# Gate products of the expert layer: sixteen tokens in one batch, and their steps as separate background tasks

## The chip, the cores and the metric

The kernel runs on one core of a Trainium2 chip. The metric is the time of one execution in device microseconds (us); lower is better. A core has TensorE (PE, matrix multiplications; PEld are its weight loads), VectorE (DVE), ScalarE (ACT), GpSimd (POOL) and SyncE (SP, which here only issues loads). Each engine works through its own list of instructions in order; semaphores join the lists.

## The reference, cut to what matters

Two blocks of a transformer run one after the other on 256 tokens of width 1024. The first block has two layers, and each of them ends in an expert layer ("peer") with 16384 experts; the change is in that one. For every token, eight heads choose 16 experts each and a softmax weight (the gate) for each.

```
hid = gelu(einsum('td,thkd->thk', tc, u[ec]))
return einsum('thk,thkd->td', gc * hid, v[ec])
```

`ec` holds the indices of the chosen experts (a number from 0 to 16383, made of two halves e1 and e2 of 7 bits each), `gc` the gates, `u` and `v` the tables of experts.

## The kernel before, in words

**The expert layer is computed densely.** All 16384 experts are multiplied, since 256 tokens choose 32768 of them in all. First the U phase: 128 tiles of `u`, each 128 experts by 1024; TensorE multiplies a tile with all 256 tokens, ScalarE applies gelu, and H (in two buffers, `Ha` and `Hb`, expert by token) stands in SBUF. Then the V phase: H is multiplied by the gates, and 128 tiles of `v` are multiplied with it and summed in four PSUM banks (`acc`).

**Every tile of weights comes the same way** (class `Weights`). SP loads 512 KB into `wraw` (three buffers), ACT rounds it to `whi` (L178), DVE subtracts to get the rest `wlo` (L179); both have three buffers, and `W.get()` of a tile first splits the tile two ahead. A product in near-fp32 precision is three matmuls, hi by hi, hi by lo, lo by hi (L320 to L322). A tile is 24 of them. In the V phase the moving operand is split as well: `gated` multiplies H of one row of experts by its gates (L1018, DVE, from a buffer `gj` that POOL fetches from DRAM), and `hg` splits it into `xh` (L333, ACT) and `xl` (L334, DVE), two tiles ahead.

**Gates.** For tokens 0 to 127 the gates are scattered to a DRAM table and fetched back (`gj`). For tokens 128 to 255 they are made on chip, and that is the function `gates(half, newps, cost)`: for every token, a one-hot matrix of e1 (`ga`, 128 wide) times a one-hot matrix of e2 scaled with the gate (`gbh` and `gbl`, the gate's high and low half in f16, 64 columns for one half of the experts). It works in groups of eight tokens, 16 groups to a half, and has three steps:

- `make(q)`: four operations on 128 x 512 or 128 x 1024 values in f16. `gb` (L965) and `ga` (L966) on DVE; `gbh` (L967) and `gbl` (L968) on DVE in half 0 and on POOL in half 1. `gb` has one buffer, the others two.
- `mult(q)`: sixteen matmuls of 64 columns (L975, L976) into a PSUM bank, on TensorE, between two weight tiles.
- `fold(q)`: DVE multiplies H by the bank (L985).

Half 0 is called in the U phase of each layer, at its tile 72, and half 1 at the start of the V phase: four stretches in the program, with 16 groups each.

**What sets the order.** A queue of background tasks, `bg`, holds pairs of a cost and a function. After each weight tile `bg.tick(rate)` adds `rate` to a credit and runs tasks while the credit is above zero, taking each one's cost from it. `rate` is the sum of all costs divided by the number of tiles to spread them over (54 in half 0, 60 in half 1). Before, a task is `step(q)` with a cost of 1.0: `mult(q-1)`, then `make(q)`, then `fold(q-2)`; there are 18 of them for 16 groups, so a step runs after every third tile, in half 1 sometimes after a fourth.

Of the kernel before, what the change touches and what calls it, by code (L numbers as in the profile page):

```python
# [248 lines left out]
def _program(tc, nc, glob, wpool, mmp, accp, drp, ins, out, scat, stop):  # L249
# [33 lines left out]
    bg = Tasks()  # L283
# [3 lines left out]
    def zero(l, src, upto):  # L287

        n = 128 * 128 // NZ
        while cleared[l] < min(upto, NZ):  # L290
            i = cleared[l]
            nc.scalar.dma_start(scat[l][:, i * n:i * n + n], src)
            cleared[l] += 1
# [19 lines left out]
    def mmtile():  # L313
        return mmp.tile([128, 512], F32, tag="mm", name="mm")
# [165 lines left out]
    def ft_tile(ps, n, cols=None, first=True, steady=True):  # L480

        hi, lo = W.get()
        if first and steady:
            settle(ps)
        for c in range(8):
            s = slice(c * 128, c * 128 + 128)
            xh_, xl_ = n.x(c, cols)
            mm3(ps, hi[:, s], lo[:, s], xh_, xl_, first and c == 0, c == 7, skip_group_check=True)
# [269 lines left out]
    def peer(l, n, close_parts, open_parts):  # L758
# [191 lines left out]
        bg.add(0.4, to_hk)  # L950


        def gates(half, newps, cost):
            st = {}

            E = nc.gpsimd if half else V

            def make(q):
                s = slice(q * 8, q * 8 + 8)
                js = slice(half * 64, half * 64 + 64)  # L960
                a = sp.tile([128, 8, 128], F16, name="ga", bufs=2)
                b = sp.tile([128, 8, 64], F16, name="gb", bufs=1)
                bh = sp.tile([128, 8, 64], F16, name="gbh", bufs=2)
                bl = sp.tile([128, 8, 64], F16, name="gbl", bufs=2)
                V.tensor_tensor(b, n8[:, None, js].to_broadcast([128, 8, 64]), e2T[:, s, None].to_broadcast([128, 8, 64]), op=ALU.is_equal)  # L965
                V.tensor_tensor(a, n8[:, None, :].to_broadcast([128, 8, 128]), e1T[:, s, None].to_broadcast([128, 8, 128]), op=ALU.is_equal)  # L966
                E.tensor_tensor(bh, b, gh[:, s, None].to_broadcast([128, 8, 64]), op=ALU.mult)  # L967
                E.tensor_tensor(bl, b, gl[:, s, None].to_broadcast([128, 8, 64]), op=ALU.mult)  # L968
                st[q] = (a, bh, bl)

            def mult(q):
                a, bh, bl = st.pop(q)
                ps = newps()
                for t in range(8):
                    T_.matmul(ps[:, t * 64:t * 64 + 64], a[:, t], bh[:, t], start=True, stop=False)  # L975
                    T_.matmul(ps[:, t * 64:t * 64 + 64], a[:, t], bl[:, t], start=False, stop=True)  # L976
                P.broken = False
                st[("p", q)] = ps

            def fold(q):  # L980
                pv = st.pop(("p", q)).rearrange("p (t j) -> p j t", t=8)
                t = slice(128 + q * 8, 128 + q * 8 + 8)
                for j0, j1 in ((0, NA), (NA, 64)) if half == 0 else ((64, 128),):
                    hv = Ha[:, j0:j1, t] if j1 <= NA else Hb[:, j0 - NA:j1 - NA, t]
                    V.scalar_tensor_tensor(hv, pv[:, j0 - half * 64:j1 - half * 64], 1.0 / GSCALE, hv, op0=ALU.mult, op1=ALU.mult)  # L985

            def step(q):
                if 0 <= q - 1 < 16:
                    mult(q - 1)
                if q < 16:  # L990
                    make(q)
                if 0 <= q - 2 < 16:
                    fold(q - 2)

            for q in range(18):
                bg.add(cost, lambda q=q: step(q))


        xn = Plain(xh, xl)
# [24 lines left out]
        def hg(upto):  # L1024
            gated(upto)
            while done[0] <= min(upto, 127):
                j = done[0]
                split(xh[:, j % 8, 0:256], xl[:, j % 8, 0:256], Ha[:, j] if j < NA else Hb[:, j - NA])
                done[0] += 1

        rate = TK_U
        for jp in range(64):
            if jp == TK_G // 2:
                bg.drain()
                gates(0, acctile, 1.0)
                rate = bg.spread(126 - TK_G)
            ps = mmtile()
            for s in range(2):
                ft_tile(ps[:, s * 256:s * 256 + 256], xn, slice(ROW - SEQ, ROW), s == 0)
                bg.tick(rate)  # L1040
            if l == 0:
                zero(1, zt, jp + 1)
            if jp == 63:
                bg.drain()
                hg(1)
            j = jp * 2
            A.activation(Haf[:, j * 256:j * 256 + 512] if j < NA else Hbf[:, (j - NA) * 256:(j - NA) * 256 + 512], ps, AF.Gelu)  # L1047


        gates(1, mmtile, 1.0)  # L1050
        rate = bg.spread(TK_V)
        acc = [acctile() for _ in range(4)]

# [501 lines left out]
    if stop == "mix0":  # L1555
        dump()
        return close_parts()
    n = peer(0, nxt, close_parts, lambda: open_parts(lambda pr, sp: Norm(("norm_mix", 1), META, pr, mmtile)))
    if stop == "peer0":
        dump()  # L1560
# [7 lines left out]
    if stop == "mix1":  # L1568
        dump()
        return close_parts()  # L1570
    n = peer(1, made["n"], close_parts, lambda: open_parts(lambda pr, sp: TwoNorms(pr, sp, mmtile), ROW))
    btp = tc.tile_pool(name="btp", bufs=1)
    sp = btp.__enter__()
# [50 lines left out]
```

## Time and profile before

| what | value |
|---|---|
| median of 3 runs | 2392.7 us (2392.18 to 2393.62) |
| the profiled execution | 2391.17 us, span of its instructions 2389.4 us |
| TensorE | busy 2362.6 us, 99% of the span, 20554 matmuls |
| VectorE | busy 1839.7 us, 77% |
| ScalarE | busy 1208.0 us, 51% |
| GpSimd | busy 644.7 us, 27% |
| granted TensorE clock | 0.998 of full speed |

TensorE is busy nearly all the time and its chain ends last: 92% of the chain of waits is TensorE's. A busy TensorE is not one at its peak, because matmuls overlap and their ends are modelled; the distance from one start to the next tells what a matmul takes. The times of the trace count from the start of the span. The four stretches with gates lie at about 399 to 547 us and 1269 to 1417 us (half 0) and at 561 to 724 us and 1431 to 1594 us (half 1).

### The profile page before, as it was taken

The page shows a single profiled execution, that of the slowest core. Times are in us where ns is not written, and L with a number is a line of the kernel's source. Part 1 is how long each engine was busy: PE and PEld are TensorE (multiplying, and loading weights), DVE is VectorE, ACT ScalarE, POOL GpSimd, SP SyncE. Part 2 cuts the span into 40 slices and gives each one's busy share as a digit, 9 for nine tenths or more (in the row PEclk, how much of TensorE's full clock was granted, in tenths as well). Part 3 has the DMA queues.
Part 4 walks back from the last instruction along what each step waited for, and adds up shares of the span by engine and source line. Part 5 has one row for each costly group of instructions (what it writes and reads, how often), then busy time and mean ns, then how long its engine had stood idle before and what let it go on. Part 6 is the DMA issues. An engine that isn't in the chain of part 4 may idle for free.

```text
span 2389.4 us, 50610 instructions
## 1 busy us (share of the span) xinstructions
PE 2362.6 (99%) x20554; PEld 2302.4 (96%) x20554; DVE 1839.7 (77%) x3518; ACT 1208.0 (51%) x1753; POOL 644.7 (27%) x421
## 2 busy tenths in 40 slices
PE   8999999999999999999999999999999999999999
PEld 6799999999999999999999999999999998789999
DVE  6689896887996668798987879986677655767774
ACT  4555555444444555555554444445565443446553
POOL 0007877812330000038878504310010000200000
PEclk9999999999999999999999999999999999999999
DMA  7578888765666665657777756666665565325655
GB/s 246 164 245 228 230 224 205 179 191 194 206 207 220 220 216 191 206 167 179 186 178 188 191 185 200 205 215 220 220 197 186 177 175 181 118 98 178 195 191 170
DMA packets 170650, 464.39 MB, mean 194 GB/s; under 512 B 52368, under 2 KB 54424, under 8 KB 169904
## 3 DMA queue, kind: packets, MB, share of 16 engines
q1 hardware_dynamic: 117440, 420.04, 54.9%
q0 software_dynamic: 43616, 24.27, 8.0%
q10 hardware_dynamic: 9360, 16.84, 1.9%
q8 instruction: 161, 2.64, 0.4%
q14 instruction: 73, 0.60, 0.1%
HBM read 443.09 MB, written 17.99 MB: 193 GB/s over the span
## 4 chain that ended last, share of the span: by engine, by line
PE 92%; DVE 6%; ACT 1%; issue 1%; DMA 1%; SPq 0%; ACTq 0%; DVEq 0%
PE mm L320 19%; PE mm L322 19%; PE mm L321 19%; PE acc L320 10%; PE acc L321 10%; PE acc L322 9%; PE acc L258 3%; PE mm L258 2%; DVE wlo L179 2%; DMA wraw<-in_mix_in 1%; PE acc L262 0%; ACT whi L178 0%; PE mm L975 0%; PE acc L975 0%; PE mm L976 0%
## 5 line engine op out<-in xcount | busy, mean ns | idle before, releaser
L179 DVE TENSOR_TENSOR wlo<-wraw,whi 128x1024 fp32r<-128x1024 f32 (+2 forms) x799 | 995.3, 1249 | 399.6 <-ACT whi L178 388.9
L178 ACT CAST whi<-wraw 128x1024 fp32r<-128x1024 f32 (+2 forms) x799 | 834.6, 1045 | 618.4 <-PE mm L321 214.4
L320 PE MATMUL mm<-xh,whi 128*128 128x256 f32 (+1 forms) x2632 | 739.1, 281 | 0.0
L322 PE MATMUL mm<-xh,wlo 128*128 128x256 f32 (+1 forms) x2632 | 732.1, 278 | 1.2 <-DVE wlo L179 1.1
L321 PE MATMUL mm<-xl,whi 128*128 128x256 f32 (+1 forms) x2632 | 731.5, 278 | 0.0
L320 PE MATMUL acc<-xh,whi 128*128 128x256 f32 x2048 | 568.6, 278 | 0.5 <-ACT xh L333 0.5
L321 PE MATMUL acc<-xl,whi 128*128 128x256 f32 x2048 | 565.8, 276 | 0.2
L322 PE MATMUL acc<-xh,wlo 128*128 128x256 f32 x2048 | 565.5, 276 | 0.0
L887 POOL DMA_INDIRECT gates<-gt,idx x256 | 483.4, 1888 | 217.8 <-DVE idx L877 94.5
L320 PEld LDWEIGHTS mm<-xh,whi 128*128 128x128 f32 x2632 | 495.1, 188 | 7.3 <-issue 6.4
L322 PEld LDWEIGHTS mm<-xh,wlo 128*128 128x128 f32 x2632 | 495.2, 188 | 2.6 <-DVE wlo L179 2.2
L321 PEld LDWEIGHTS mm<-xl,whi 128*128 128x128 f32 x2632 | 497.6, 189 | 0.0
L320 PEld LDWEIGHTS acc<-xh,whi 128*128 128x128 f32 x2048 | 384.5, 188 | 0.9 <-ACT xh L333 0.9
L321 PEld LDWEIGHTS acc<-xl,whi 128*128 128x128 f32 x2048 | 384.7, 188 | 0.5 <-DVE xl L334 0.5
L322 PEld LDWEIGHTS acc<-xh,wlo 128*128 128x128 f32 x2048 | 384.5, 188 | 0.0
L322 PE MATMUL mm<-ph,wlo 128*128 128x256 f32 (+1 forms) x800 | 226.1, 283 | 4.3 <-DVE wlo L179 4.3
L320 PE MATMUL mm<-ph,whi 128*128 128x256 f32 (+1 forms) x800 | 227.1, 284 | 0.0
L321 PE MATMUL mm<-pl,whi 128*128 128x256 f32 (+1 forms) x800 | 225.8, 282 | 0.0
L322 PEld LDWEIGHTS mm<-ph,wlo 128*128 128x128 f32 x800 | 151.1, 189 | 4.7 <-DVE wlo L179 4.7
L321 PEld LDWEIGHTS mm<-pl,whi 128*128 128x128 f32 x800 | 151.6, 190 | 0.3
L320 PEld LDWEIGHTS mm<-ph,whi 128*128 128x128 f32 x800 | 151.3, 189 | 0.1
L1047 ACT ACTIVATE Hb<-mm 128x512 f32<-128x512 f32 x112 | 67.0, 598 | 164.8 <-PE mm L322 154.6
(333 smaller groups left out, 3027.3 us busy)
## 6 DMA issues: line engine op xcount, KB each, us to landing
wraw<-in_u SPq DMA_DIRECT2D x256, 512.0 KB
wraw<-in_v SPq DMA_DIRECT2D x256, 512.0 KB
wraw<-in_ffn_in SPq DMA_DIRECT2D x88, 512.0 KB
wraw<-in_mix_in SPq DMA_DIRECT2D x52, 512.0 KB
gates<-zt ACTq DMA_DIRECT2D x64, 256.0 KB
wraw<-in_wq SPq DMA_DIRECT2D x32, 512.0 KB
gj<-gates POOLq DMA_DIRECT2D x64, 256.0 KB
wraw<-in_ffn_out SPq DMA_DIRECT2D x32, 512.0 KB
```

The lines of the kernel that those rows point to most:

```text
L178: self.nc.scalar.copy(hi[:, :cols], raw[:, :cols])
L179: self.nc.vector.tensor_tensor(lo[:, :cols], raw[:, :cols], hi[:, :cols].bitcast(F32), op=ALU.subtract)
L258: return T_.matmul(*a, **k)
L320: T_.matmul(ps, wh, mh, start=start, stop=False, **kw)
L321: T_.matmul(ps, wh, ml, start=False, stop=False, **kw)
L322: T_.matmul(ps, wl, mh, start=False, stop=stop, **kw)
L887: b = nc.gpsimd.indirect_dma_start(out=flat, out_offset=bass.IndirectOffsetOnAxis(ap=idx[:, i:i + 1], axis=0), in_=gt0[:, i:i + 1], in_off ...
L1047: A.activation(Haf[:, j * 256:j * 256 + 512] if j < NA else Hbf[:, (j - NA) * 256:(j - NA) * 256 + 512], ps, AF.Gelu)
```

## The change

`gates` loses its parameter `cost`, and `step` is gone. Groups go in pairs: five tasks for two groups, with costs of their own (0.5, 0.8, 0.3, 0.2, 0.2; 2.0 for a pair and 16 for a half). Both `mult` of a pair stand in one task, so their 32 matmuls follow each other. The sizes of the operations, the buffers and the engines stay as they are.

```
-        def gates(half, newps, cost):
+        def gates(half, newps):
...
-            def step(q):
-                if 0 <= q - 1 < 16:
-                    mult(q - 1)
-                if q < 16:
-                    make(q)
-                if 0 <= q - 2 < 16:
-                    fold(q - 2)
-
-            for q in range(18):
-                bg.add(cost, lambda q=q: step(q))
+            for q in range(0, 16, 2):
+                bg.add(0.5, lambda q=q: make(q))
+                bg.add(0.8, lambda q=q: make(q + 1))
+                bg.add(0.3, lambda q=q: (mult(q), mult(q + 1)))
+                bg.add(0.2, lambda q=q: fold(q))
+                bg.add(0.2, lambda q=q: fold(q + 1))
...
-                gates(0, acctile, 1.0)
+                gates(0, acctile)
...
-        gates(1, mmtile, 1.0)
+        gates(1, mmtile)
```

The lines below `step` move up by four: L1018 of before is L1014 now.

VectorE in the V phase, half 1, before: one whole step and the tiles up to the next one (`gb` and `ga` make a group, L985 folds an older one, then a tile's own L1018, L179 and L334 follow).

```order
L965 TENSOR_TENSOR gb<-n_1331,e2T 128x512
L966 TENSOR_TENSOR ga<-n_1331,e1T 128x1024
L985 SCALAR_TENSOR_TENSOR Hb<-mm,Hb 128x64x8
L1018 TENSOR_TENSOR Ha<-Ha,gj 128x128
L179 TENSOR_TENSOR wlo<-wraw,whi 128x1024
L334 TENSOR_TENSOR xl<-Ha,xh 128x256
```

VectorE at the same stage now, in the third pair of the half.

```order
L965 TENSOR_TENSOR gb<-n_1331,e2T 128x512
L966 TENSOR_TENSOR ga<-n_1331,e1T 128x1024
L1014 TENSOR_TENSOR Hb<-Hb,gj 128x128
L179 TENSOR_TENSOR wlo<-wraw,whi 128x1024
L334 TENSOR_TENSOR xl<-Hb,xh 128x256
L965 TENSOR_TENSOR gb<-n_1331,e2T 128x512
L966 TENSOR_TENSOR ga<-n_1331,e1T 128x1024
L1014 TENSOR_TENSOR Hb<-Hb,gj 128x128
L179 TENSOR_TENSOR wlo<-wraw,whi 128x1024
L334 TENSOR_TENSOR xl<-Hb,xh 128x256
```

The second `make` now stands one tile behind the first, and no fold stands behind `ga`. In half 1 this is so in four of the eight pairs of a layer; in the other four there are two tiles between the makes. From one pair to the next there are seven or eight tiles. `mult` of a pair stands three tiles behind the second `make` (in half 0 twice only two), the folds one or two tiles behind `mult`. In half 0 the makes of a pair stand one tile apart in four pairs and two tiles apart in four.

GpSimd at the start of half 1, before: a fetch of `gj` stands between the products of two groups.

```order
L967 TENSOR_TENSOR gbh<-gb,gh 128x512
L968 TENSOR_TENSOR gbl<-gb,gl 128x512
L1008 DMA gj<-gates 128x512
L967 TENSOR_TENSOR gbh<-gb,gh 128x512
L968 TENSOR_TENSOR gbl<-gb,gl 128x512
```

GpSimd at the same place now.

```order
L967 TENSOR_TENSOR gbh<-gb,gh 128x512
L968 TENSOR_TENSOR gbl<-gb,gl 128x512
L967 TENSOR_TENSOR gbh<-gb,gh 128x512
L968 TENSOR_TENSOR gbl<-gb,gl 128x512
L1004 DMA gj<-gates 128x512 x2
```

The products of a pair follow each other, and the fetches stand behind both.

## Rows read from the trace of the kernel before

**Rows 1.** The page, part 1: busy us, share of the span, instructions.
```profile
PE 2362.6 (99%) x20554; PEld 2302.4 (96%) x20554; DVE 1839.7 (77%) x3518; ACT 1208.0 (51%) x1753; POOL 644.7 (27%) x421
```

**Rows 2.** PE's waits, all of those for wlo: total us, times, longest.
```profile
PE mm L322 <- DVE wlo L179: 5.4, 5, 2.1
```

**Rows 3.** Timeline of PE, first matmuls behind a gate batch: start, us, operation.
```profile
407.68 0.37 PE L320 MATMUL mm<-xh,whi 128*128 128x256 f32 x1
407.88 0.28 PE L321 MATMUL mm<-xl,whi 128*128 128x256 f32 x1
```

**Rows 4.** Timeline of DVE (start, us), first step of half 1: no fold.
```profile
561.54 0.68 DVE L965 TENSOR_TENSOR gb<-n,e2T 128x512 f16<-128x512 f16 x1
...
563.28 1.13 DVE L1018 TENSOR_TENSOR Ha<-Ha,gj 128x128 f32<-128x128 f32 x1
564.33 2.06 DVE L179 TENSOR_TENSOR wlo<-wraw,whi 128x1024 fp32r<-128x1024 f32 x1
566.31 0.41 DVE L334 TENSOR_TENSOR xl<-Ha,xh 128x256 fp32r<-128x256 f32 x1
566.65 0.28 DVE L1018 TENSOR_TENSOR Ha<-Ha,gj 128x128 f32<-128x128 f32 x1
```

**Rows 5.** Timeline of POOL: products of the first two groups of half 1.
```profile
562.40 1.86 POOL L967 TENSOR_TENSOR gbh<-gb,gh 128x512 f16<-128x512 f16 x1 [69.18 <-DVE gb L965]
564.23 1.08 POOL L968 TENSOR_TENSOR gbl<-gb,gl 128x512 f16<-128x512 f16 x1
...
570.83 3.75 POOL L967 TENSOR_TENSOR gbh<-gb,gh 128x512 f16<-128x512 f16 x1 [5.00 <-PE mm L976]
574.55 1.03 POOL L968 TENSOR_TENSOR gbl<-gb,gl 128x512 f16<-128x512 f16 x1
```

**Rows 6.** Timeline of DVE, second step of half 1: no fold behind it.
```profile
569.99 0.68 DVE L965 TENSOR_TENSOR gb<-n,e2T 128x512 f16<-128x512 f16 x1
...
571.73 0.28 DVE L1018 TENSOR_TENSOR Ha<-Ha,gj 128x128 f32<-128x128 f32 x1
...
573.07 0.42 DVE L334 TENSOR_TENSOR xl<-Ha,xh 128x256 fp32r<-128x256 f32 x1
573.40 0.28 DVE L1018 TENSOR_TENSOR Ha<-Ha,gj 128x128 f32<-128x128 f32 x1
574.62 2.05 DVE L179 TENSOR_TENSOR wlo<-wraw,whi 128x1024 fp32r<-128x1024 f32 x1 [0.93 <-ACT whi L178]
```

**Rows 7.** Timeline of DVE, a later step, with its fold.
```profile
590.27 0.69 DVE L965 TENSOR_TENSOR gb<-n,e2T 128x512 f16<-128x512 f16 x1
...
592.01 0.68 DVE L985 SCALAR_TENSOR_TENSOR Hb<-mm,Hb 128x512 f32<-128x512 f32 x1
...
595.04 0.41 DVE L334 TENSOR_TENSOR xl<-Ha,xh 128x256 fp32r<-128x256 f32 x1
```

**Rows 8.** Timeline of PE: the first use of the xl of rows 7.
```profile
596.43 0.28 PE L321 MATMUL acc<-xl,whi 128*128 128x256 f32 x1
```

**Rows 9.** Timeline of ACT, a V tile without gates: its whi.
```profile
734.55 1.05 ACT L178 CAST whi<-wraw 128x1024 fp32r<-128x1024 f32 x1 [1.36 <-PE acc L321]
```

**Rows 10.** Timeline of DVE, V tiles without gates.
```profile
736.78 0.42 DVE L334 TENSOR_TENSOR xl<-Hb,xh 128x256 fp32r<-128x256 f32 x1
737.11 0.28 DVE L1018 TENSOR_TENSOR Hb<-Hb,gj 128x128 f32<-128x128 f32 x1
738.35 1.23 DVE L179 TENSOR_TENSOR wlo<-wraw,whi 128x1024 fp32r<-128x1024 f32 x1 [0.95 <-ACT whi L178]
739.50 0.42 DVE L334 TENSOR_TENSOR xl<-Hb,xh 128x256 fp32r<-128x256 f32 x1
```

**Rows 11.** Busy time of a half-1 stretch: PE, PEld, DVE, ACT, POOL, clock, DMA.
```profile
560.00:720.00 160.00, 160.00 (x1585) 159.41 (x1584) 149.18 (x213) 78.27 (x112) 56.14 (x46) 1.00 0.64 205
```

**Rows 12.** Timeline of DVE, U phase: a make without a fold.
```profile
399.23 0.69 DVE L965 TENSOR_TENSOR gb<-n,e2T 128x512 f16<-128x512 f16 x1
...
402.17 2.58 DVE L179 TENSOR_TENSOR wlo<-wraw,whi 128x1024 fp32r<-128x1024 f32 x2
```

## The prediction, made before the changed kernel was run

> **What bounds the kernel now.** I read the page's busy times first, then TensorE's waits, then the timelines of TensorE, VectorE and GpSimd in the four stretches with gates. TensorE is busy for 99% of the span [rows 1], and its waits for `wlo` come to 5.4 us in all [rows 2]; none of them lies in a gate stretch. So time is won only by taking work from TensorE, and lost as soon as an operand of the next tile comes too late. The reader is to see how much room there is for that. In half 1 VectorE is busy 149.2 of 160 us [rows 11], and in a tile of 24 matmuls everything is due at a fixed point.
>
> **How late VectorE may be.** A V tile takes 2.72 us (L334 of one tile to the next, 736.78 to 739.50 [rows 10]). ACT's `whi` starts when TensorE frees its buffer, some 0.13 us into a tile that starts at 734.42 [rows 9]. Call this tile 0. Its program position makes `xl` of tile 2, which ends at 736.78 + 0.42 = 737.20, so 2.78 us after the start of tile 0. Tile 2 starts 5.44 us after it and reads `xl` with its second matmul, 0.11 later. The room is 5.55 - 2.78 = 2.8 us. A regular step before uses most of it: from rows 7, `xl` ends at 595.04 + 0.41 = 595.45, and its first use is at 596.43 [rows 8]; 0.98 us are left. A step is followed by two or three tiles without one, each of which gives back some 1.05 us (2.72 less the 1.67 us that L1018, L179 and L334 take, 571.73 to 573.40 [rows 6]), so nothing ever waits.
>
> **The change part by part.**
>
> *What it removes.* A batch of 64-column matmuls has a cost of its own where it ends: the first weight matmul behind it takes 0.20 us to the next start (407.68 to 407.88 [rows 3]) where one takes 2.72 / 24 = 0.113 elsewhere. That is 0.09 us, and 64 batches become 32: 32 x 0.09 = **-2.9 us**. The matmuls themselves stay. All operations on the other engines stay too, in number and size.
>
> *What it moves, half 1.* Two makes stand close together, and no fold stands behind `ga`. The price of such a make is seen twice in the trace, and the two differ.
>
> - First step of half 1: `gb` starts at 561.54, and L1018 of the next tile at 566.65, so a make and the tile's own work take 5.11 us; `xl` ends at 566.31 + 0.41, 5.18 us after `gb` [rows 4]. Without a make that is 1.67. L1018 takes 1.13 instead of 0.28 and `wlo` 2.06 instead of 1.23: each stands while one of GpSimd's products runs (562.40 to 564.26 and 564.23 to 565.31 [rows 5]).
> - Second step: 569.99 to 573.40 is 3.41 us, `xl` ends 3.50 us after `gb` [rows 6], and nothing is slow. GpSimd's `gbh` takes 3.75 us instead [rows 5]: it gets on only when VectorE pauses at 573.7, and `wlo` behind the pause is slow (2.05).
>
> So VectorE and GpSimd exclude each other here, and a make costs 1.74 us on VectorE and about 1.7 us more, at once or later. In a step with a fold 0.60 of it runs beside the fold, which does not stand still (0.68 [rows 7], its usual time).
>
> The Trainium skill, page "SBUF — State Buffer", section "Who interferes with whom", says that a VectorE instruction with two SBUF inputs and a GpSimd instruction that reads SBUF exclude each other for a whole instruction, and that the one issued first goes first. By that rule GpSimd would go first in every pair, as in rows 4. Rows 6 disagree: `gbh` was issued at 570.83, and four VectorE instructions issued after it passed.
>
> I take rows 4 for the forecast: GpSimd's second product got in directly behind L1018 in the first step too, and in every regular step (all have a slow `wlo`); rows 6 are the exception.
>
> Pairs one tile apart (four in a layer): the first `gb` starts with the tasks of tile 0, at 737.11 - 734.42 = 2.69. The second stands 5.11 later, at 7.80. The `xl` behind it ends 5.18 later, at 12.98; it belongs to tile 4, due at 10.88 + 0.11 = 10.99. TensorE waits **2.0 us**.
>
> Pairs two tiles apart (four in a layer): two folds stand one tile ahead; their 1.2 us, with the 0.20 of L1018, overrun the 1.24 between L1018 and the next `wlo` (737.11 to 738.35 [rows 10]), which makes the start some 0.16 late: 2.85. Then 5.11 and a plain tile of 1.67 give 9.63, `xl` ends at 14.81, due at 13.60 + 0.11. TensorE waits **1.1 us**.
>
> After the wait there are seven or eight tiles at 1.05 us of gain each to the next pair, so lateness doesn't add up. The sum of half 1 is 2 layers x (4 x 2.0 + 4 x 1.1) = **+24.8 us**.
>
> The bounds of this. Below: where GpSimd finds pauses and VectorE pays 1.74 a make, `xl` of a close pair ends at 2.69 + 3.41 + 3.50 = 9.6, before 10.99, and nothing waits: 0. Above: the order of rows 6 in every second make. The second `gb` needs the buffer of the first, so VectorE stands until both products are through (573.40 to 575.58, 2.2 us [rows 5, 6]): second `gb` at 2.69 + 3.41 + 2.2 = 8.3, `xl` ends at 11.8, 0.8 late. Then GpSimd waits for VectorE's next pause, which comes only after it has caught up, some three tiles of 1.67 on, at about 16; the products end at 18. `mult` is due behind tile 4, at 13.6 + 0.8 = 14.4, so TensorE waits 3 us or more there. That makes 3.8 a close pair and about 2.8 a wide one, 2 x (4 x 3.8 + 4 x 2.8) = 53 us.
>
> *GpSimd's queue.* The fetch of `gj` now stands behind both products of a pair. It is issued four tiles (10.9 us) before its use; two makes hold it up by some 5 us in rows 4's order. I cost it at nothing; with rows 6's order the cover is nearly gone, which is part of the 53.
>
> *What it moves, half 0.* All four operations of a make are VectorE's: 2.94 us (399.23 to 402.17 [rows 12]). Two makes (5.88) and two `wlo` (1.14 each) are 8.2 us against three tiles of 8.16. Depending on where gelu delays `whi`, a close pair is just in time or 0.2 late. I take **+0.5 us** (bounds 0 and 2). `mult` of a pair comes at least two tiles (5.4 us) behind the second make, against 2.94 of work; the folds stand behind `mult` by at least a tile, whose `wlo` can't start earlier than `mult` does. Both cost nothing.
>
> *The sum.* 2391.2 of the profiled execution - 2.9 + 24.8 + 0.5 = 2413.6. The median is 1.5 above that execution, so **2415 us**, some 0.9% slower.
>
> **The rivals.**
>
> 1. *GpSimd starves* (rows 6 in most second makes): 2391.2 - 2.9 + 53 + 0.5 = 2442, at the median 2443. For it speaks that the second step is the nearer likeness, with GpSimd already at work in the half; against it that the other hand-overs went to GpSimd.
> 2. *Not slower.* GpSimd's products run wholly in VectorE's pauses and beside folds, and the second `gb` finds its buffer free. Then only the 2.9 us are left: 2390. It decides at the second `gb`: it holds if VectorE has paused 2.2 us between the two makes. The pauses of a plain tile are 0.95 us [rows 10]; a close pair has one tile between, a wide one two. So this speaks against it.
> 3. *A part of it.* The order changes from pair to pair so that the wide pairs lose nothing and the close ones 1 to 1.5 us: 2 x 4 x 1.2 = 10, so 2400. For it speaks that DVE idles and DMA landings move the phase between pairs.
>
> **How the numbers follow.** What can't be told from no change here is 0.2%, 4.8 us. Forecast 2415 (rows 4's order): 0.50, its own range 2407 to 2424. Rival 1: 0.25. Rival 3: 0.14. Rival 2: 0.11; of that 0.08 within 0.2%, 0.03 faster by more, since 2.9 us is all that the trace shows to be won. The range for 8 times in 10 is 2398 to 2441: from just below rival 3 to about rival 1. Slower by over 0.2%: 0.89.
>
> **What would show it.** 32 batches of 32 matmuls with one slow first matmul behind each. In half 1, TensorE waits eight times per layer of 1 to 2 us, for `xl` of the fourth tile that starts behind a close pair's first make and the fifth behind a wide pair's; L1018 and `wlo` at 1.13 and 2.06 behind both makes of a pair. Half 0 with next to no waits. Rival 1 would show in `gbh` of over 3 us and waits at L975 for GpSimd. The prediction is wrong if TensorE runs through the close pairs without a wait, or if the loss lies in half 0 or outside the four stretches.

## The result, and the profile after

The changed kernel takes 2426.2 us (median, 2423.32 to 2428.16), the kernel before 2392.44 (2390.41 to 2393.62) in the runs beside it: ratio 1.0141, interval 1.0127 to 1.0155. Forecast were 2415 us and a range of 2398 to 2441: slower as forecast, within the range, and 11 us more than the value. The profiled executions took 2427.13 us (span 2425.4) and 2391.17 (span 2389.4), so 36.0 us are to be explained.

Part 1 of the page after (busy us, share of the span, instructions):

```profile
PE 2376.2 (98%) x20554; PEld 2313.0 (95%) x20554; DVE 1853.7 (76%) x3518; ACT 1205.1 (50%) x1753; POOL 672.4 (28%) x421
```

The counts are those of before [rows 1]: nothing was added or left out. The first three of TensorE's waits of after (total us, times, longest):

```profile
PE acc L321 <- DVE xl L334: 19.2, 16, 1.5
PE mm L258 <- ACT whi L178: 9.8, 1, 9.8
PE mm L322 <- DVE wlo L179: 5.2, 4, 2.1
```

The last line is [rows 2] again, and the middle one stood in the kernel before with 8.2 us. The first is new: sixteen waits for `xl`, eight in each layer, all in half 1. Where the time went is read from ACT's `whi` of two fixed tiles, the fourth and the 65th of the V phase of the first layer (the first starts beside the first make, the second when the last pair is through). In the kernel before (start, us):

```profile
561.74 1.05 ACT L178 CAST whi<-wraw 128x1024 fp32r<-128x1024 f32 x1 [1.41 <-issue]
...
737.27 1.05 ACT L178 CAST whi<-wraw 128x1024 fp32r<-128x1024 f32 x1 [1.36 <-PE acc L321]
```

and after:

```profile
562.42 1.06 ACT L178 CAST whi<-wraw 128x1024 fp32r<-128x1024 f32 x1 [1.33 <-issue]
...
753.95 1.05 ACT L178 CAST whi<-wraw 128x1024 fp32r<-128x1024 f32 x1 [1.36 <-PE acc L321]
```

175.53 us became 191.53: 16.0 us lost in half 1 of the first layer. The same two tiles of the second layer give 175.69 us (from 1431.50) and 193.25 (from 1449.18), 17.6 more. Together 33.6 of the 36.0 us. Half 0 (a `whi` at its start and at its end) became 0.4 and 0.2 us shorter; the other 2.9 lie outside the gate stretches, 1.6 of them in the one wait for `whi` at the start of the kernel (9.8 for 8.2).

VectorE in the first close pair of half 1, after; its answer before is [rows 4], and for a second make [rows 6]:

```profile
562.30 0.69 DVE L965 TENSOR_TENSOR gb<-n,e2T 128x512 f16<-128x512 f16 x1
...
567.41 0.68 DVE L965 TENSOR_TENSOR gb<-n,e2T 128x512 f16<-128x512 f16 x1
568.01 1.21 DVE L966 TENSOR_TENSOR ga<-n,e1T 128x1024 f16<-128x1024 f16 x1
569.15 1.13 DVE L1014 TENSOR_TENSOR Ha<-Ha,gj 128x128 f32<-128x128 f32 x1
570.20 2.06 DVE L179 TENSOR_TENSOR wlo<-wraw,whi 128x1024 fp32r<-128x1024 f32 x1
572.17 0.41 DVE L334 TENSOR_TENSOR xl<-Ha,xh 128x256 fp32r<-128x256 f32 x1
572.51 0.28 DVE L1014 TENSOR_TENSOR Ha<-Ha,gj 128x128 f32<-128x128 f32 x1
```

From `gb` to `gb` 5.11 us, L1014 at 1.13 and `wlo` at 2.06 behind both makes: [rows 4] twice, as forecast. `xl` ends 5.17 us behind the second `gb`, at 572.58. TensorE at that place:

```profile
570.34 0.28 PE L322 MATMUL acc<-xh,wlo 128*128 128x256 f32 x1
570.76 0.38 PE L320 MATMUL acc<-xh,whi 128*128 128x256 f32 x1
572.64 0.39 PE L321 MATMUL acc<-xl,whi 128*128 128x256 f32 x1 [1.49 <-DVE xl L334]
572.86 0.28 PE L322 MATMUL acc<-xh,wlo 128*128 128x256 f32 x1
```

The starts should be 0.113 apart. They are 0.42 and 1.88 apart: 0.31 + 1.77 = 2.1 us of wait, and the start behind it (0.22) is 0.11 late too. In wide pairs the wait is 1.15 (one of them 0.49), in the first close pair of the second layer 1.7. The starts over these tiles of both layers add up to 24.5 us of waits; 2.0 was forecast for a close pair and 1.1 for a wide one, 24.8 in all.

Most of the rest is a thing the forecast did not hold. TensorE behind the third close pair (matmuls that start after a wait which ended at 665.38):

```profile
666.41 0.28 PE L320 MATMUL acc<-xh,whi 128*128 128x256 f32 x1
666.52 0.34 PE L321 MATMUL acc<-xl,whi 128*128 128x256 f32 x1
666.66 0.42 PE L322 MATMUL acc<-xh,wlo 128*128 128x256 f32 x1
666.87 0.42 PE L320 MATMUL acc<-xh,whi 128*128 128x256 f32 x1
667.09 0.41 PE L321 MATMUL acc<-xl,whi 128*128 128x256 f32 x1
```

Starts go from 0.11 to 0.21 apart and stay so into the next gate batch, which begins at 669.44; from 666.6 to 670.0 the granted clock is 0.50. The busy times of this stretch and of that behind the fourth close pair (PE, PEld, DVE, ACT, POOL, then the granted clock; [rows 11] has 1.00):

```profile
660.00:680.00 20.00, 18.39 (x168) 17.90 (x168) 15.94 (x25) 8.24 (x12) 3.63 (x4) 0.91 0.50 174
700.00:720.00 20.00, 18.39 (x168) 17.91 (x167) 17.70 (x25) 8.25 (x12) 6.93 (x6) 0.91 0.56 180
```

TensorE ran at 1.2 GHz for some 3.4 us, behind two of the four close pairs of the first layer and three of four in the second. The slow matmuls there are 7.7 us longer in sum.

### The profile page after: what moved, and what is told of

Its sections match the earlier page's. It is cut to its first block, busy times and chain, and to the rows that moved or that the text cites. A ratio compares the mean times of both kernels' runs of the same rounds, so it can differ in the third digit from the quotient of the medians.

```text
span 2425.4 us, 50606 instructions
## 1 busy us (share of the span) xinstructions
PE 2376.2 (98%) x20554; PEld 2313.0 (95%) x20554; DVE 1853.7 (76%) x3518; ACT 1205.1 (50%) x1753; POOL 672.4 (28%) x421
## 4 chain that ended last, share of the span: by engine, by line
PE 86%; DVE 10%; issue 2%; ACT 1%; DMA 1%; SPq 0%; ACTq 0%; DVEq 0%
PE mm L320 19%; PE mm L322 19%; PE mm L321 18%; PE acc L321 8%; PE acc L320 8%; PE acc L322 8%; DVE wlo L179 3%; PE acc L258 3%; PE mm L258 2%; DVE ga L966 1%; DVE xl L334 1%; DVE Hb L1014 1%; ACT whi L178 1%; DVE gb L965 1%; DMA wraw<-in_mix_in 1%
## 5 line engine op out<-in xcount | busy, mean ns | idle before, releaser
L179 DVE TENSOR_TENSOR wlo<-wraw,whi 128x1024 fp32r<-128x1024 f32 (+2 forms) x799 | 992.5, 1247 | 420.2 <-ACT whi L178 405.3
L321 PE MATMUL acc<-xl,whi 128*128 128x256 f32 x2048 | 571.4, 279 | 19.3 <-DVE xl L334 19.2
L887 POOL DMA_INDIRECT gates<-gt,idx x256 | 492.8, 1925 | 214.8 <-DVE idx L877 94.9
L967 POOL TENSOR_TENSOR gbh<-gb,gh 128x512 f16<-128x512 f16 x32 | 75.3, 2352 | 282.6 <-DVE gb L965 280.5
```

Source lines behind the costliest of these rows:

```text
L179: self.nc.vector.tensor_tensor(lo[:, :cols], raw[:, :cols], hi[:, :cols].bitcast(F32), op=ALU.subtract)
L321: T_.matmul(ps, wh, ml, start=False, stop=False, **kw)
L887: b = nc.gpsimd.indirect_dma_start(out=flat, out_offset=bass.IndirectOffsetOnAxis(ap=idx[:, i:i + 1], axis=0), in_=gt0[:, i:i + 1], in_off ...
```

## The experiments

The theory: makes one or two tiles apart cost VectorE more than the room of 2.8 us, since each stands about 1.7 us for GpSimd's products; `xl` comes late; TensorE waits, and then may run at 1.2 GHz for a while. The rivals: the batch of 32 products costs by itself; VectorE's own comparisons, or the order of the tasks, would do it without GpSimd; and the slow stretches come by chance. "Half 1" below is by how much the V tiles that the gates run beside take longer than in the kernel before, both layers together, in the profiled executions (the changed kernel: + 33.6 us).

**1. The makes spread, the products still together.**

```
-  bg.add(0.5, lambda q=q: make(q))
-  bg.add(0.8, lambda q=q: make(q + 1))
-  bg.add(0.3, lambda q=q: (mult(q), mult(q + 1)))
+  bg.add(0.85, lambda q=q: make(q))
+  bg.add(0.85, lambda q=q: make(q + 1))
+  bg.add(0.1, lambda q=q: (mult(q), mult(q + 1)))
-  bg.add(0.2, lambda q=q: fold(q))
-  bg.add(0.2, lambda q=q: fold(q + 1))
+  bg.add(0.1, lambda q=q: fold(q))
+  bg.add(0.1, lambda q=q: fold(q + 1))
```

> The two makes of a pair stand three or four tiles apart in half 1 (two to four in half 0); the products of sixteen tokens still come together. Theory (a make costs VectorE about 3.44 us beside the tile's own work, and two close ones overrun the 2.8 us of room): a make's lateness is nearly given back before the next, so the 1.15 and 2.0 us waits for xl go; a rest of at most 0.5 us per pair is left, because a pair with its two folds (2 x 3.44 + 2 x 0.6 = 8.1 us) is about what some 7.3 tiles give back (7.7 us). No stretch at the 1.2 GHz level in half 1. Time 2389 to 2397. Rival (the batch of 32 products, or the tasks' being split, is itself what costs): stays at 2420 to 2428.

Ratio to the kernel before 1.0017 (1.0008 to 1.0027), 2397.15 us beside 2392.27; half 1 + 5.4. Its waits:

```profile
PE acc L321 <- DVE xl L334: 2.5, 6, 0.7
```

Six waits of 2.5 us in all stand where the changed kernel has sixteen of 19.2. With batches of 32 as in the changed kernel, the loss is nearly gone: it was the distance of the makes. No slow stretch in half 1. The time is 0.15 us above the range that was expected, and the longest waits (0.8 us by the starts) above the 0.5 expected.

**2. Without GpSimd's products in half 1** (left out as the expectation says; the order stays).

```
-  V.tensor_tensor(b, n8[:, None, js].to_broadcast([128, 8, 64]), e2T[:, s, None].to_broadcast([128, 8, 64]), op=ALU.is_equal)
+  V.tensor_tensor(bh if half else b, n8[:, None, js].to_broadcast([128, 8, 64]), e2T[:, s, None].to_broadcast([128, 8, 64]), op=ALU.is_equal)
...
+  if half:
+      st[q] = (a, bh, bh)
+      return
```

> Left out: GpSimd's two products of half 1 (the one-hot factor goes into both matmuls as it is). Order of VectorE's and TensorE's instructions as in the changed kernel. Theory (the second half of a make's price is VectorE standing while GpSimd's products run): a make costs 1.74 us, ga and wlo of half 1 fall to their usual 0.9 and 1.2 us, no wait for xl; time about 2390 (2387 to 2394). Rival (VectorE's own two comparisons, two makes one tile apart, overrun the room by themselves): waits stay over 1 us and the time at 2405 or above.

Ratio 0.9985 (0.9974 to 0.9995), 2389.12 us; half 1 - 2.2. VectorE in the first close pair:

```profile
561.73 0.68 DVE L965 TENSOR_TENSOR gbh<-n,e2T 128x512 f16<-128x512 f16 x1
562.34 1.22 DVE L966 TENSOR_TENSOR ga<-n,e1T 128x1024 f16<-128x1024 f16 x1
563.47 0.29 DVE L1017 TENSOR_TENSOR Ha<-Ha,gj 128x128 f32<-128x128 f32 x1
563.68 1.22 DVE L179 TENSOR_TENSOR wlo<-wraw,whi 128x1024 fp32r<-128x1024 f32 x1
564.81 0.42 DVE L334 TENSOR_TENSOR xl<-Ha,xh 128x256 fp32r<-128x256 f32 x1
565.15 0.69 DVE L965 TENSOR_TENSOR gbh<-n,e2T 128x512 f16<-128x512 f16 x1
```

From make to make 3.42 us, not 5.11: the missing 1.69 is what GpSimd's products cost VectorE, and L1017 and `wlo` are back at 0.29 and 1.22. No wait for `xl` is left, though makes are as close as before. So VectorE's own share (1.74 a make) fits the room, and the 1.69 does not.

**3. Half 1's products on VectorE.**

```
-            E = nc.gpsimd if half else V
+            E = V
```

> Half 1's two products move from GpSimd to VectorE. Theory: a make costs VectorE 2.94 us (as in half 0) in place of 3.44. Close pair: xl ends at 2.69 + 2.94 + 1.67 + 2.94 + 1.74 = 11.98 against 10.99, a wait of 1.0; wide pair 0.1. 2 x (4 x 1.0 + 4 x 0.1) = 8.8 us over a kernel without waits (2390): 2399, fewer or no stretches at 1.2 GHz. Rival (VectorE is full in half 1, so anything given to it costs more than GpSimd's exclusion): over 2426.

Ratio 1.0046 (1.0031 to 1.006), 2402.84 us; half 1 + 10.3. That is 4 us above the 2399 expected, but the waits are those worked out: every close pair but the first of the second layer (0.70) waits 0.92 at the start that needs `xl`, 1.1 with the start ahead of it, for 1.0. VectorE does 2.94 us of work a make in place of 1.74, and the kernel is 1% faster than the changed one all the same: what counts is how long `xl` is held up, not which engine is busy. No slow stretch behind a wait of 0.92.

**4. The products of a pair as two tasks.**

```
-  bg.add(0.3, lambda q=q: (mult(q), mult(q + 1)))
+  bg.add(0.15, lambda q=q: mult(q))
+  bg.add(0.15, lambda q=q: mult(q + 1))
```

> The two batches of a pair are tasks of their own (eight tokens each, 64 batches as before the change); makes and folds stay where the changed kernel has them. Theory (the loss is the makes' closeness, the pairing of products a gain of about 3 us): waits of 1.15 and 2.0 us unchanged, 32 more batch ends; 2427 to 2431. Rival (the long batch of 32 is what makes operands late, or what pulls the clock down): falls below 2418.

Ratio 1.0144 (1.0119 to 1.017), 2427.3 us; half 1 + 33.7. The joint batch is not the cause: apart, it costs the same. Its waits are fewer, and it pays more for the clock (seven slow stretches, one behind nearly every close pair):

```profile
PE acc L321 <- DVE xl L334: 14.5, 11, 1.5
PE mm L976 <- POOL gbl L968: 2.4, 3, 0.8
```

**5. The wait filled with work.** To tell idle time from chance as the cause of the slow stretches.

```
+  if j in (4, 19, 34, 49):
+      k = ident.bitcast(F16)
+      for _ in range(15):
+          T_.matmul(acc[0][:, 0:256], k[:, 0:256:2], k, start=False, stop=False, skip_group_check=True)
   for m in range(8):
       vmm(j, m, part, m, j == 0, False)
```

> The changed kernel, with 15 added f16 matmuls of 256 columns (weights of zeros, so nothing is added to the result) ahead of the first matmul of V tiles 4, 19, 34 and 49, the four tiles of a layer that wait 2.0 us for xl. They run inside the wait (15 x 0.107 = 1.6 us, an estimate from 256 columns at 2.4 GHz). Theory (the part of the loss that the sum of waits doesn't hold is TensorE's fall to 1.2 GHz behind the 2.0 us waits, because it stood idle): no stretch at 1.2 GHz behind these tiles, and the time falls by about 8 us, to 2415 to 2421, though work was added. Rival (the falls have nothing to do with the idle time; they come with the load or by chance): stretches stay, time 2425 or above.

Ratio 1.0097 (1.0082 to 1.0113), 2415.34 us beside 2390.54: faster than the changed kernel by 0.4%, with 120 matmuls more. TensorE at the fourth close pair (start, us, operation):

```profile
709.08 0.28 PE L322 MATMUL acc<-xh,wlo 128*128 128x256 f32 x1
709.19 1.81 PE L1071 MATMUL acc<-ident 128*128 128x256 f16 x15
710.76 0.36 PE L320 MATMUL acc<-xh,whi 128*128 128x256 f32 x1
711.35 0.39 PE L321 MATMUL acc<-xl,whi 128*128 128x256 f32 x1 [0.22 <-DVE xl L334]
```

And the busy times where the changed kernel had a granted clock of 0.91:

```profile
660.00:680.00 20.00, 19.78 (x197) 19.35 (x196) 17.52 (x26) 8.96 (x14) 5.58 (x4) 1.00 0.59 198
700.00:720.00 20.00, 19.78 (x198) 19.36 (x197) 17.55 (x23) 8.26 (x12) 6.93 (x6) 1.00 0.56 190
```

The `xl` matmul starts as late as ever (2.27 us behind the last one of the tile before, as in the same pair of the changed kernel), but the clock stays at 1.00 and no slow stretch is left in half 1: + 26.7 in place of + 33.6, so the slow stretches were worth 6.9 us there. The mean granted clock says the same of all four executions: 0.999 to 1.000 here, 0.993 to 0.995 in the changed kernel's four. Of the 11.4 us between the two spans 4.5 lie elsewhere; among other things, two slow stretches outside half 1 (at 172 and 1056 us of the changed kernel's trace) are missing here. Such single ones are in the kernel before too (104, 1039, 2111). Chance is part of the clock's account: this run still has three waits of 1.8 to 2.3 us in which nothing was filled in (at 170, 642 and 1051 us), and none of them is followed by a slow stretch. But eight close pairs without one, in each of four executions by the clock, are more than chance.

**6. All pairs two tiles apart.**

```
-  bg.add(0.5, lambda q=q: make(q))
-  bg.add(0.8, lambda q=q: make(q + 1))
+  bg.add(0.64, lambda q=q: make(q))
+  bg.add(0.66, lambda q=q: make(q + 1))
```

> All eight pairs of a half stand two tiles apart, none one. Theory (a wait is what two makes overrun the room by, a tile more gives back 1.05 us, and 1.15 us of idle time doesn't bring TensorE's clock down): 16 waits of 1.15 us and 16 slower starts of 0.11 behind them, 20.2 us over a kernel without waits (2389): 2409, within 2406 to 2412, no stretch at 1.2 GHz in half 1. Rival (waits are a matter of phase, not of distance): waits of 2.0 us stay among them, time over 2415.

A miss: ratio 1.0152 (1.0133 to 1.017), 2429.18 us; half 1 + 43.5 in the profiled execution (2438.7 us, the slowest of the five). The rival named there (waits of 2.0 us for `xl`) is not it either, though: one such wait is left. TensorE at the first pair:

```profile
577.71 0.19 PE L975 MATMUL mm<-gbh,ga 128*128 128x64 f16 x1 [1.58 <-POOL gbh L967]
579.69 0.21 PE L976 MATMUL mm<-gbl,ga 128*128 128x64 f16 x1 [1.79 <-POOL gbl L968]
```

It waits for both products. GpSimd there (start, us, operation):

```profile
565.48 1.86 POOL L967 TENSOR_TENSOR gbh<-gb,gh 128x512 f16<-128x512 f16 x1 [67.88 <-DVE gb L965]
...
572.24 5.42 POOL L967 TENSOR_TENSOR gbh<-gb,gh 128x512 f16<-128x512 f16 x1 [3.32 <-DVE gb L965]
577.62 2.02 POOL L968 TENSOR_TENSOR gbl<-gb,gl 128x512 f16<-128x512 f16 x1
```

Here the order of [rows 6] came up in the second make: VectorE went on without a pause, `gbh` took 5.42 us, VectorE lost nothing, and `mult`, which this schedule puts two tiles behind the second make in these pairs, waited 1.7 and 1.95 us. That is rival 1 of the prediction, at its price (3 us or more). It happens in six of the sixteen pairs, and each of the six has a slow stretch in or behind its wait.

**7. The same, with the products a tile later.**

```
-  bg.add(0.66, lambda q=q: make(q + 1))
-  bg.add(0.3, lambda q=q: (mult(q), mult(q + 1)))
-  bg.add(0.2, lambda q=q: fold(q))
-  bg.add(0.2, lambda q=q: fold(q + 1))
+  bg.add(0.9, lambda q=q: make(q + 1))
+  bg.add(0.26, lambda q=q: (mult(q), mult(q + 1)))
+  bg.add(0.1, lambda q=q: fold(q))
+  bg.add(0.1, lambda q=q: fold(q + 1))
```

> As the kernel with all pairs two tiles apart, with the products of a pair one tile later (three or four tiles behind the second make, in place of two or three). Theory (in a wide pair one make goes each way; where the second is the one in which VectorE goes on and gbh stands for 5.4 us, both products are through 8.1 us behind the make, and the two waits for them, 3.7 us together, came only from products that were due 2.72 us too soon): of these waits some 1 us for gbl is left, 8 times, beside 8 waits of 0.5 to 1.15 us for xl; no stretch at 1.2 GHz in half 1; 2389 + 8 x 1.0 + 8 x 1.1 + 1.8 = 2408, within 2403 to 2412. Rival (GpSimd gets on only when TensorE waits and so leaves VectorE without work, so that later products only move the wait): waits of 3.7 us stay and the time at 2420 or above.

Ratio 1.0069 (1.0045 to 1.0094), 2413.15 us beside 2394.17; 1 us above the range expected; half 1 + 17.8. The long waits for products are gone but for about 1 us three times and 0.4 once:

```profile
PE acc L321 <- DVE xl L334: 5.4, 6, 1.5
PE mm L976 <- POOL gbl L968: 2.6, 4, 0.8
PE acc L320 <- ACT xh L333: 2.5, 4, 1.3
```

So they were due too soon, as the theory said. In two pairs TensorE still stands for 2.6 and 3.2 us (waits for `xh` and `xl`), and one slow stretch is left in half 1. The time goes from 2403.16 to 2415.47 in its four executions: with makes this close, the schedule alone does not settle it.

**8. Makes where they were, products of sixteen tokens together.** Each make but the first three of a half has a fold beside it, now that of three groups back; the products are a task of their own.

```
 for q in range(0, 16, 2):
+    if q:
+        bg.add(0.3, lambda q=q: (mult(q - 2), mult(q - 1)))
+    bg.add(1.0, lambda q=q: (make(q), q > 2 and fold(q - 3)))
+    bg.add(0.7, lambda q=q: (make(q + 1), q > 1 and fold(q - 2)))
+bg.add(0.3, lambda: (mult(14), mult(15)))
+for i in (13, 14, 15):
+    bg.add(0.6, lambda i=i: fold(i))
```

> Makes stay where the kernel before has them, a fold beside each (now that of three groups back); the products of two groups come together in a task of their own, one tile ahead of an even make. Theory (only the makes' closeness and the folds' leaving them cost; the long batch gains 0.1 us for each batch end that goes): no waits in half 1, 32 batches of 1.04 us in place of 64 of 0.57; 2.9 to 3.3 us below the kernel before, 2389, ratio 0.9987. Rival (coming together costs something of its own, such as ga's two buffers being freed late, so that VectorE's ga waits for TensorE): not below the kernel before, 2393 or more.

Ratio 0.9988 (0.9979 to 0.9997), 2388.34 us beside 2390.54: the only version with the full computation that beats the kernel before, by 0.12%, as worked out. In half 1 it waits once:

```profile
PE mm L976 <- POOL gbl L968: 0.8, 1, 0.8
```

That is a make with no fold beside it, whose `gbh` took 3.75 us. The gain in the first layer's half 1 is 0.7 us, eight batch ends at 0.09; in the second, the one wait takes it back.

## Why the prediction was right, and what it missed

**Batch ends, -2.9.** Right. The first weight matmul behind a batch still takes 0.20 us to the next start (412.23 to 412.43, as 407.68 to 407.88 [rows 3]); there are 32 of them in place of 64:

```profile
412.23 0.37 PE L320 MATMUL mm<-xh,whi 128*128 128x256 f32 x1
412.43 0.28 PE L321 MATMUL mm<-xl,whi 128*128 128x256 f32 x1
```

Run 8 shows the gain by itself.

**Half 1, +24.8.** Right in place, order and size: 24.5 us of waits, close pairs 2.0 to 2.1 (once 1.7) for 2.0, wide pairs 1.15 (once 0.49) for 1.1. "A make costs 1.74 on VectorE and about 1.7 us more" is shown by run 2 (3.42 in place of 5.11), and the room of 2.8 us by run 3, whose wait comes from the same sum with another price. Two things came out otherwise than told. In wide pairs it is the first make whose `gbh` starves (3.76 us), and GpSimd gets on in a slow `wlo` and `xl` a tile later; from `gb` to `gb` that makes 6.78 us, the very 5.11 + 1.67 of the sum, so the order changed and the price did not. The first wide pair:

```profile
585.54 3.76 POOL L967 TENSOR_TENSOR gbh<-gb,gh 128x512 f16<-128x512 f16 x1 [8.57 <-DVE gb L965]
588.52 1.86 DVE L179 TENSOR_TENSOR wlo<-wraw,whi 128x1024 fp32r<-128x1024 f32 x1
590.31 1.26 DVE L334 TENSOR_TENSOR xl<-Ha,xh 128x256 fp32r<-128x256 f32 x1
```

Since wide pairs lost 1.15, rival 3 (2400), for which they had to lose nothing, is out.

**Half 0, +0.5, and GpSimd's queue, nothing.** Right as far as can be read: with its own batch ends half 0 was forecast 0.95 us shorter in both layers together, and became 0.5 shorter. No wait over 0.15 us lies there.

**The term that was missing** holds most of the 11 us: the sum took each wait at its length and ended at the operand's arrival. Behind it two more things happened. The next start is late as well, 0.11 us sixteen times, 1.7 us in all. And TensorE, having stood for 2.0 us, ran at 1.2 GHz for some 3.4 us behind five of eight close pairs: 7.7 us by the slow starts, 6.9 by run 5, which took only the idle time away. With 24.5 of waits and 1.4 less for half 1's own batch ends, 24.5 + 1.7 + 7.7 - 1.4 = 32.5 of the 33.6. Most of what is left are starts 0.118 us apart in place of 0.113, at a granted clock of 1.00: in the 200 us from the start of each V phase 344 of them for 159 before, 0.8 us more. With the missing term the forecast would have been about 2424.

The clock was in the rows read ([rows 11]: 1.00), but as a state, not as something that a wait could change. The trace of the kernel before had a case of it. The longest wait of [rows 2] ends at 1038.14, and 1.2 us later the granted clock is 0.50 (the first row is the start behind the wait, the second the busy times of the stretch, the clock third from the end):

```profile
1038.14 0.39 PE L322 MATMUL mm<-ph,wlo 128*128 128x256 f32 x1 [2.13 <-DVE wlo L179]
1039.30:1042.70 3.40, 3.40 (x19) 3.40 (x18) 3.33 (x10) 2.04 (x4) 0.00 (x0) 0.50 0.80 270
```

Its twin in the first layer, at 170 us, is as long and has no slow stretch behind it.

**The range.** The time lies 2 us above the forecast's own range (2407 to 2424). It lies within 2398 to 2441 because rival 1 had stretched that one upwards, and not because the cost of the clock was foreseen; that much was luck.

**A reading that was wrong** without touching the sum: [rows 2] are not all of TensorE's waits for `wlo` in the kernel before. There are 2.7 us more at another line (L258), and the longest wait of all is one of 8.2 us for `whi`; none of them lies in a gate stretch.

**Rival 1** (GpSimd starves) did not decide the changed kernel: its `gbh` is over 3 us in one make of four (the first of each wide pair) and nobody waits for it there. Run 6 shows how near it was: one tile less to `mult`, and it decides. **Rival 2** (not slower) failed where it was said to decide, at the second make.

**The rule weighed** (the Trainium skill, page "SBUF — State Buffer", section "Who interferes with whom": VectorE instructions with two SBUF inputs and GpSimd instructions that read SBUF exclude each other, and the one issued first goes first). This case agrees with the first half: without GpSimd's products (run 2) L1017 takes 0.29 us for 1.13 and `wlo` 1.22 for 2.06. Who goes first is not what the rule says: in run 6 seven VectorE instructions (573.14 to 576.48) started behind the start of the `gbh` of 5.42 us (572.24) and ended before it did, as four did in [rows 6].

## What to carry to other kernels

Before moving work on a helper engine together, work out how late the engine may be at the next fixed use, and price the moved work with what the other engine's work beside it takes away. Look at the next due time too: in run 6 one tile more between the makes left the products one tile less. Price a wait of TensorE by more than its length: look at what the granted clock does behind it, and if a wait can't be avoided, see whether work can stand in it. A joint batch is worth having only where the operations that feed it can stay where they were.

## What the runs showed of the hardware that was not expected

- Added work made the kernel faster: 120 matmuls in waits that existed anyway took 0.4% off (2426.2 to 2415.3 us), and no slow stretch was left in half 1.
- Idle times of 0.9 to 1.2 us were never followed by a slow stretch in half 1 (runs 3, 6, the wide pairs); of about 2 us, by one in five of eight cases in the changed kernel and in seven of eight in run 4. Outside half 1 every one of these ten traces has two waits of 2.3 to 2.6 us for `wlo` (near 170 and 1050 us); 15 of the 20 are followed by one, or overlap it. What tells the cases apart is open.
- Which of VectorE and GpSimd goes first: a make with a fold (one PSUM operand) right beside it always had its `gbh` at 1.9 us: behind `ga` in the kernel before (28 of 28) and in run 8 (26 of 26), ahead of `gb` in runs 1 (14 of 14) and 7 (8 of 8). Without one, 1.9 to 2.1 and 3.8 to 7.1 us both occur. What decides then is open; it wasn't tried by itself.
- Starts of TensorE's 256-column matmuls lie 0.113 us apart, but in stretches of every trace here 0.118, at a granted clock of 1.00. In run 1 this makes some 2 us of the 5.4 in half 1. What sets it the runs don't show.
